# Moving the last two tiles' elementwise work of each up half from GpSimd to VectorE, placing the first down weights' low parts behind them, and reordering the last row scalings

## The chip, the core and the metric

The kernel runs on one core of a Trainium2 chip. The core has a matrix engine (TensorE, PE in the profile, with its weight loads listed as PEld), three engines for elementwise work (VectorE = DVE, ScalarE = ACT, GpSimd = POOL) and SyncE (SP), which here only issues transfers. Each engine works through its own queue in order; semaphores tie the queues together. The metric is the device time of one execution in microseconds. Three runs of the kernel before gave 871.04 us as their median (870.61 to 871.61).

## The reference: what is computed

One encoder block on a sequence of 512 tokens of width 1024, in float32: three token mixers merged by gates, then a feed-forward part and a final norm. The change touches the feed-forward part and the end:

```python
def conv_glu_ffn(h, w_up, w_conv, b_conv, w_down):
    a, u = jnp.split(h @ w_up, 2, axis=-1)
    return (jax.nn.gelu(dwconv3(a, w_conv, b_conv)) * u) @ w_down
...
        x = x + conv_glu_ffn(rms_norm(x, ffn_norm_g[l]), w_ffn_up[l], w_ffn_conv[l], b_ffn_conv[l], w_ffn_down[l])
    return rms_norm(x, final_norm_g)
```

`w_up` is 1024 x 5632 (2816 channels for `a`, 2816 for `u`), `w_down` is 2816 x 1024. `dwconv3` is a convolution of three taps along the tokens, channel by channel.

## The kernel before

**Products in three parts.** Every matrix product of float32 operands is made of three products of shorter numbers: each operand is split into a high part (ScalarE rounds it, line 242 for weights, 1304 for activations) and a low part (VectorE subtracts the high part, line 243 for weights, 1305 for activations). High by high, high by low and low by high are added up in PSUM: lines 260, 261, 262 where a weight is the stationary operand, lines 1255, 1256, 1257 in the down product.

**Weights.** They come as blocks of 128 x 1024 in the order of a list. SyncE loads a block into one of three `raw` buffers (`wr`, line 206). `emit_split` (line 223) splits it in two halves of 512 columns into four `hi` (`wh`) and four `lo` (`wl`) buffers. `weights(key)` splits one block ahead of the one it hands out and loads three ahead.

**The up half.** The 2816 channels are 22 tiles of 128, handled in two halves (`hh`) of 11 tiles (`j` = 0 to 10). For each tile TensorE makes the `a` product (24 matmuls of 512 columns) and then the `u` product (24 more). Meanwhile the other engines work on the `a` tile in a chain. `conv` multiplies it out of PSUM into a padded buffer (line 518, `pad`, the tile's first operation), and then come the three taps (line 520 on ACT, 521 and 522 on DVE). The gelu follows (1347 ACT, 1348 DVE, 1349 ACT, 1350 DVE), and then a multiplication by the rows' norm factor (line 1351), on GpSimd for the tiles 0 to 9 and on VectorE for tile 10. When the `u` product stands in PSUM, `gated` multiplies the two (line 1358, DVE), splits a half of the result (1304, 1305) and forms differences and sums of the two halves of the tokens: line 1361 in the first half, lines 1365, 1367 and 1368 in the second, all on GpSimd. The last tile's `gated` is put behind the first block of the down product that follows.

**The down products.** Seven products of half size (a scheme of the Strassen kind: B11 and T3 after the first half, B21, T1, T2, B22 and T4 after the second) each run over 11 tiles `k` of 128 channels and two groups of 128 tokens, with three matmuls of 512 columns each: 66 matmuls. One half block of weights, `wh` and `wl`, serves one `k`, which is six matmuls. B21 is the first product behind the second up half. Its weight blocks 0, 1 and 2 hold the tiles `k` = 0 and 1, 2 and 3, 4 and 5.

**The end.** T4 is the last product. While it runs, row groups 0 and 1 of the output are scaled and written (`finish`: a small addition at line 1286, a power at 1287 on GpSimd, two scalings at 1293 on VectorE, a transfer at 1300). With `hold=5`, T4 puts the last 15 matmuls on the bank of row group 3, so group 2's bank is complete before. Behind T4 come group 2 (line 1412 adds the bank, 1271 squares it on ACT, 1286, 1287, two scalings at 1293, transfer at 1417) and group 3 (1271, 1286, 1287, then 1421 on DVE and 1423 on ACT, with transfers at 1422 and 1424).

**Order.** Tile programs are queued engine by engine by a scheduler that works from the order of the code, readiness and explicit edges; `tc.issue_after(x)` keeps what a block emits on `x`'s engine behind `x` in that engine's queue, without a wait for its end.

Of the kernel before, what the change touches and what calls it, by code (L numbers as in the profile page):

```python
# [14 lines left out]
ALU = mybir.AluOpType  # L15
# [3 lines left out]
S = 512  # L19
D = 1024  # L20
# [5 lines left out]
HF = FT // 2  # L26
# [72 lines left out]
BLOCKS = block_list()  # L99
# [22 lines left out]
def hybrid_block(ctx, tc, xg, xT, memT, wflat, vecs, gbias, nabias, out):  # L122
# [99 lines left out]

    def emit_split(i):
        key, n = BLOCKS[i]
        r = raws.pop(i)
# [288 lines left out]
    def conv(ps, rbt, w, b, i, n):  # L514

        pad = pads[npad[0] % 2]
        npad[0] += 1
        V.tensor_tensor(pad[:, 1:513], ps, rbt, op=ALU.mult)  # L518
        t1 = scr()
# [798 lines left out]
    for hh in range(2):  # L1318
# [6 lines left out]
        for j in range(HF):  # L1325
# [24 lines left out]
            V.scalar_tensor_tensor(c, sq, 1.0, c, op0=ALU.add, op1=ALU.mult)  # L1350
            (V if j == HF - 1 else G).tensor_tensor(c, c, rb2, op=ALU.mult)  # L1351
            if f > 0:
                pu = pu1 if f == 1 else proj(("uu", f), HH, HL)

            def gated(j=j, pu=pu, c=c):

                r, q = (r1 if hh else r0)[j], r0[j]
                V.scalar_tensor_tensor(r, pu, 0.5, c, op0=ALU.mult, op1=ALU.mult)  # L1358
                if hh == 0:
                    split_half(a11, j, r[:, one_])  # L1360
                    G.tensor_tensor(r[:, one_], r[:, two_], r[:, one_], op=ALU.subtract)
                    late.append(lambda: split_half(s3, j, r[:, one_]))
                else:
                    split_half(a12, j, r[:, one_])
                    G.tensor_tensor(q[:, two_], q[:, two_], r[:, two_], op=ALU.subtract)
                    late.append(lambda: split_half(s1, j, q[:, two_]))
                    G.tensor_tensor(q[:, one_], q[:, one_], r[:, two_], op=ALU.subtract)
                    G.tensor_tensor(r[:, one_], r[:, one_], q[:, one_], op=ALU.add)

# [33 lines left out]
    def last_residual():  # L1403
# [4 lines left out]
        1: [lambda: gather(pc, 0, 1, ALU.add), lambda: ready(1, 0, 1)],  # L1408
        2: [last_residual],
        3: [lambda: finish(0, vs[0])],  # L1410
        4: [lambda: finish(1, vs[1]), lambda: V.tensor_tensor(cv(3, 1), cv(3, 1), gfin[:, S:D], op=ALU.mult)]})
    V.tensor_tensor(cv(2, 0), cv(2, 0), pa_[0], op=ALU.add)
    squares(cv(2, 0), 2, 0)
    col = power(2, vs[2], 0)
    scaled(2, 1, col)
    scaled(2, 0, col)
    SY.dma_start(out[2 * P:3 * P, :], C[1][:, :D])
    squares(pa_[1], 3, 0)
    col = power(3, vs[3], 0)
    oa, ob = scr(), scr()  # L1420
# [112 lines left out]
```

## Time and profile before

| | us |
|---|---|
| median of three runs | 871.04 (870.61 to 871.61) |
| the profiled execution, its own time | 870.92 |
| span of the profiled execution | 869.1 |
| busy: PE / DVE / ACT / POOL | 859.1 / 629.0 / 481.1 / 174.3 |
| second up half, its 11 tiles' first operations (line 518) | 667.22 to 781.49 |
| B21 / T1 begin on PE | 781.26 / 801.14 |
| last matmul begins | 861.66 |

The span is that of the engines' records; 1.82 us of the profiled execution's own time lie around it. TensorE is busy for 99% of the span, so time is to be had where it waits, where its clock is lowered, and behind the last matmul. A row of the timeline gives start, duration, engine, line, operation, the tiles written and read, and in brackets how long the engine was idle before and what ended that. Between matmuls in a row the starts lie 0.227 us apart though each is listed with 0.39 us, since they overlap.

### The profile page before, as it was taken

How to read it: one execution, taken by the hardware profiler on the slowest of the kernel's cores; microseconds unless marked ns; L12 is line 12 of the kernel's file. 1: busy time of each engine (PE TensorE's matmuls, PEld its weight loads, DVE VectorE, ACT ScalarE, POOL GpSimd, SP SyncE). 2: the span in 40 equal slices, each digit the busy share in tenths (PEclk: the TensorE clock that was granted, in tenths of full speed). 3: DMA queues.
4: the chain of work that ended last, by engine and by line, in shares of the span. 5: the costliest groups of instructions: out<-in, count | busy, mean ns of one | idle time of the engine just before them, and what ended most of it. 6: DMA issues, size and time to landing. Idle time of an engine off the chain costs nothing.

```text
span 869.1 us, 12209 instructions
## 1 busy us (share of the span) xinstructions
PE 859.1 (99%) x4175; PEld 722.8 (83%) x4175; DVE 629.0 (72%) x1255; ACT 481.1 (55%) x1023; POOL 174.3 (20%) x288
## 2 busy tenths in 40 slices
PE   9999999999999999999999999999999999998996
PEld 7898889988888888888888888888888888886885
DVE  7694687775567758898667549777776777777785
ACT  7363457654546658888634445555454444445763
POOL 0101100001013593700002103222200333331001
PEclk9999999999999999999999999999999999999998
DMA  7324633524485655633338956455556322225563
GB/s 277 100 74 141 205 127 116 190 86 134 158 194 130 206 157 155 165 112 110 108 99 208 326 167 146 161 178 148 145 180 194 97 98 80 91 97 183 186 204 141
DMA packets 42222, 131.93 MB, mean 152 GB/s; under 512 B 6376, under 2 KB 11496, under 8 KB 40560
## 3 DMA queue, kind: packets, MB, share of 16 engines
q1 hardware_dynamic: 32384, 101.37, 35.1%
q0 software_dynamic: 9344, 29.39, 14.0%
q8 instruction: 33, 0.54, 0.3%
q10 hardware_dynamic: 432, 0.39, 0.1%
q14 instruction: 29, 0.24, 0.1%
HBM read 126.91 MB, written 27.28 MB: 177 GB/s over the span
## 4 chain that ended last, share of the span: by engine, by line
PE 92%; DVE 3%; ACT 1%; POOL 1%; issue 1%; DMA 1%; POOLq 0%; DVEq 0%
PE mm L262 23%; PE mm L260 23%; PE mm L261 23%; PE at L1257 2%; PE at L1255 2%; PE at L1256 2%; PE at L261 2%; PE at L260 2%; PE at L262 2%; PE mm L1256 1%; PE mm L1257 1%; PE mm L1255 1%; PE at L934 1%; PE at L787 1%; PE at L915 1%
## 5 line engine op out<-in xcount | busy, mean ns | idle before, releaser
L260 PE MATMUL mm<-u,wh 128*128 128x512 f32 (+1 forms) x907 | 353.9, 390 | 0.0
L262 PE MATMUL mm<-u,wl 128*128 128x512 f32 (+1 forms) x907 | 350.2, 386 | 0.0
L261 PE MATMUL mm<-u,wh 128*128 128x512 f32 (+1 forms) x907 | 349.7, 386 | 0.0
L242 ACT ACTIVATE wh<-wr 128x512 fp32r<-128x512 f32 (+2 forms) x328 | 202.5, 624 | 167.4 <-PE mm L261 101.1
L243 DVE TENSOR_TENSOR wl<-wr,wh 128x512 fp32r<-128x512 f32 (+2 forms) x330 | 237.8, 724 | 73.6 <-ACT wh L242 69.7
L262 PEld LDWEIGHTS mm<-u,wl 128*128 128x128 f32 x907 | 170.4, 188 | 34.6
L261 PEld LDWEIGHTS mm<-u,wh 128*128 128x128 f32 x907 | 170.6, 188 | 32.8
L260 PEld LDWEIGHTS mm<-u,wh 128*128 128x128 f32 x907 | 170.5, 188 | 32.2
L600 POOL DMA_DIRECT2D u<-nav_d x128 | 62.8, 539 | 28.2 <-PE at L934 17.2
L1351 POOL TENSOR_TENSOR s<-s,rb 128x512 f32<-128x512 f32 x20 | 32.9, 1644 | 124.6 <-DVE s L1350 117.6
L169 POOL COPY y<-wl 128x1 f32<-128x1 f32 x24 | 6.9, 288 | 203.5 <-DVE wl L243 203.4
L1255 PE MATMUL at<-wh,u 128*128 128x512 f32 x100 | 39.3, 393 | 0.0
L1257 PE MATMUL at<-wh,u 128*128 128x512 f32 x100 | 38.9, 389 | 0.0
L1256 PE MATMUL at<-wl,u 128*128 128x512 f32 x100 | 38.9, 389 | 0.0
L1304 ACT ACTIVATE u<-r 128x256 fp32r<-128x256 f32 x44 | 17.7, 414 | 37.9 <-DVE r L1358 22.8
L520 ACT ACTIVATE s<-pad,vec 128x512 f32<-128x512 f32 x30 | 24.4, 812 | 17.5 <-DVE pad L518 16.8
L521 DVE SCALAR_TENSOR_TENSOR s<-pad,vec,s 128x512 f32<-128x512 f32 x30 | 22.9, 762 | 5.9 <-ACT s L520 5.8
L1347 ACT ACTIVATE s<-s 128x512 f32<-128x512 f32 x22 | 13.9, 633 | 21.7 <-DVE s L522 21.7
L1305 DVE TENSOR_TENSOR u<-r,u 128x256 fp32r<-128x256 f32 x44 | 21.0, 487 | 6.6 <-ACT u L1304 6.6
L1350 DVE SCALAR_TENSOR_TENSOR s<-s,s 128x512 f32<-128x512 f32 x22 | 15.2, 691 | 14.0 <-ACT s L1349 14.0
L522 DVE SCALAR_TENSOR_TENSOR s<-pad,vec,s 128x512 f32<-128x512 f32 x30 | 22.5, 751 | 0.8
L1349 ACT ACTIVATE s<-s 128x512 f32<-128x512 f32 x22 | 13.9, 632 | 15.5 <-DVE s L1348 15.4
(319 smaller groups left out, 1250.6 us busy)
## 6 DMA issues: line engine op xcount, KB each, us to landing
wr<-wflat SPq DMA_DIRECT2D x140, 512.0 KB, 3.4
wr<-wsum_T SPq DMA_DIRECT2D x20, 512.0 KB, 4.0
wsum_T<-wflat POOLq DMA_DIRECT2D x8, 1024.0 KB, 10.5
wsum_T<-wflat POOLq DMA_DIRECT2D x6, 768.0 KB, 7.5
nab<-nabias SPq DMA_DIRECT2D x16, 256.0 KB, 2.7
u<-nav_d POOLq DMA_DIRECT2D x128, 32.0 KB, 2.8
s<-xT SPq DMA_DIRECT2D x15, 256.0 KB, 4.7
nav_d<-nv POOLq DMA_DIRECT2D x8, 256.0 KB, 2.5
```

The costliest lines, as they stand in the source:

```text
L242: st["hi"] = A.activation(h[:, u:v], src, AF.Copy).ins
L243: st["lo"] = V.tensor_tensor(l[:, u:v], src, h[:, u:v].bitcast(F32), op=ALU.subtract).ins
L260: PE.matmul(ps, lh, rh, start=start, stop=False)
L261: PE.matmul(ps, lh, rl, start=False, stop=False)
L262: st["mm"] = PE.matmul(ps, ll, rh, start=False, stop=stop).ins
L520: A.activation(t1, pad[:, 0:512], AF.Identity, scale=vcol(w, i), bias=vcol(b, i))
L521: V.scalar_tensor_tensor(t1, pad[:, 1:513], vcol(w, n + i), t1, op0=ALU.mult, op1=ALU.add)
L600: G.dma_start(vw[r * 32:(r + 1) * 32, i * 256:(i + 1) * 256], nav_v[hf, r, CW[b]:CW[b] + 32, hp * 256:(hp + 1) * 256])
L1255: PE.matmul(bank, ah[:, ts], w[0], start=start, stop=False, skip_group_check=True)
L1256: PE.matmul(bank, ah[:, ts], w[1], start=False, stop=False, skip_group_check=True)
L1257: PE.matmul(bank, al[:, ts], w[0], start=False, stop=True, skip_group_check=True)
L1351: (V if j == HF - 1 else G).tensor_tensor(c, c, rb2, op=ALU.mult)
```

## The change

Three edits.

First, in both halves the tiles 9 and 10 do all their elementwise work on VectorE: the multiplication by the norm factor (tile 10 had it there), and the differences and sums in `gated`, one instruction a tile in the first half, three in the second.

Second, the weight blocks 0 of B11 and of B21 are split under `issue_after` of the newest `pad` instruction. At that point it is that of tile 10, so both low parts of the block stand behind it in VectorE's queue.

Third, near the end `finish(0)` and `finish(1)` stand one weight block of T4 earlier, and the squares and the small addition of row group 3 are written ahead of the second scaling of group 2, which is kept behind that addition.

```diff
     def emit_split(i):
+        if BLOCKS[i][0] in (("dn", "B11", 0), ("dn", "B21", 0)):
+            with tc.issue_after(st["pad"]):
+                split_block(i)
+        else:
+            split_block(i)
+
+    def split_block(i):
         key, n = BLOCKS[i]
...
-        V.tensor_tensor(pad[:, 1:513], ps, rbt, op=ALU.mult)
+        st["pad"] = V.tensor_tensor(pad[:, 1:513], ps, rbt, op=ALU.mult).ins
...
-            (V if j == HF - 1 else G).tensor_tensor(c, c, rb2, op=ALU.mult)
+            ve = V if j >= HF - 2 else G
+            ve.tensor_tensor(c, c, rb2, op=ALU.mult)
...
                 if hh == 0:
                     split_half(a11, j, r[:, one_])
-                    G.tensor_tensor(r[:, one_], r[:, two_], r[:, one_], op=ALU.subtract)
+                    ve.tensor_tensor(r[:, one_], r[:, two_], r[:, one_], op=ALU.subtract)
                     late.append(lambda: split_half(s3, j, r[:, one_]))
                 else:
                     split_half(a12, j, r[:, one_])
-                    G.tensor_tensor(q[:, two_], q[:, two_], r[:, two_], op=ALU.subtract)
+                    ve.tensor_tensor(q[:, two_], q[:, two_], r[:, two_], op=ALU.subtract)
                     late.append(lambda: split_half(s1, j, q[:, two_]))
-                    G.tensor_tensor(q[:, one_], q[:, one_], r[:, two_], op=ALU.subtract)
-                    G.tensor_tensor(r[:, one_], r[:, one_], q[:, one_], op=ALU.add)
+                    ve.tensor_tensor(q[:, one_], q[:, one_], r[:, two_], op=ALU.subtract)
+                    ve.tensor_tensor(r[:, one_], r[:, one_], q[:, one_], op=ALU.add)
...
-        2: [last_residual],
-        3: [lambda: finish(0, vs[0])],
-        4: [lambda: finish(1, vs[1]), lambda: V.tensor_tensor(cv(3, 1), cv(3, 1), gfin[:, S:D], op=ALU.mult)]})
+        2: [last_residual, lambda: finish(0, vs[0])],
+        3: [lambda: finish(1, vs[1])],
+        4: [lambda: V.tensor_tensor(cv(3, 1), cv(3, 1), gfin[:, S:D], op=ALU.mult)]})
     V.tensor_tensor(cv(2, 0), cv(2, 0), pa_[0], op=ALU.add)
     squares(cv(2, 0), 2, 0)
-    col = power(2, vs[2], 0)
-    scaled(2, 1, col)
-    scaled(2, 0, col)
+    col2 = power(2, vs[2], 0)
+    scaled(2, 1, col2)
+    squares(pa_[1], 3, 0)
+    col = tiny(1)
+    first = V.tensor_tensor(col, ss[3][:, 0:1], vs[3], op=ALU.add).ins
+    G.tensor_tensor(col, col, nhalf[:, :1], op=ALU.pow)
+    with tc.issue_after(first):
+        scaled(2, 0, col2)
     SY.dma_start(out[2 * P:3 * P, :], C[1][:, :D])
-    squares(pa_[1], 3, 0)
-    col = power(3, vs[3], 0)
```

The new lines shift the numbers: line 243 of before is 250 after, 518 is 525, 1305 is 1312, 1348 and 1350 are 1355 and 1357, 1351 is 1359, 1358 is 1366, 1365, 1367 and 1368 are 1373, 1375 and 1376, 1286 is 1293, 1293 is 1300, 1411 and 1412 are 1419 and 1420, 1421 is 1432.

The order of the instructions on TensorE and SyncE is the same in both kernels. Three places on VectorE show what moves. The first is VectorE's queue of before, at the end of tile 9 and the start of tile 10 of the second half (`mm_7709` is tile 9's `u` product, `mm_7750` tile 10's `a` product, `wl_7791` and `wl_7795` are the low parts of B21's block 0):

```order
L243 TENSOR_TENSOR wl_7747<-wr_7651,wh_7746 128x512
L1358 SCALAR_TENSOR_TENSOR u_6838<-mm_7709,s_7689 128x512
L1305 TENSOR_TENSOR u_6841<-u_6838,u_6841 128x256
L1305 TENSOR_TENSOR u_6844<-r_5536,u_6844 128x256
L243 TENSOR_TENSOR wl_7791<-wr_7699,wh_7790 128x512
L518 TENSOR_TENSOR pad_153<-mm_7750,rb_5621 128x512
L243 TENSOR_TENSOR wl_7795<-wr_7699,wh_7794 128x512
```

The same place after the change:

```order
L1359 TENSOR_TENSOR s_7689<-s_7689,rb_5621 128x512
L250 TENSOR_TENSOR wl_7747<-wr_7651,wh_7746 128x512
L1366 SCALAR_TENSOR_TENSOR u_6838<-mm_7709,s_7689 128x512
L1373 TENSOR_TENSOR r_5536<-r_5536,u_6838 128x256
L1375 TENSOR_TENSOR r_5536<-r_5536,u_6838 128x256
L1312 TENSOR_TENSOR u_6841<-u_6838,u_6841 128x256
L1376 TENSOR_TENSOR u_6838<-u_6838,r_5536 128x256
L1312 TENSOR_TENSOR u_6844<-r_5536,u_6844 128x256
L525 TENSOR_TENSOR pad_153<-mm_7750,rb_5621 128x512
L250 TENSOR_TENSOR wl_7791<-wr_7699,wh_7790 128x512
L250 TENSOR_TENSOR wl_7795<-wr_7699,wh_7794 128x512
```

Four instructions have come over from GpSimd, and `wl_7791` has moved from ahead of the `pad` instruction to behind it. On ScalarE one row has moved here: the high part `wh_7790` now stands between the two of line 1304.

The second place is VectorE's queue some rows further on, inside tile 10's chain, before (`wl_7835` and `wl_7839` are the low parts of B21's tiles `k` = 2 and 3, `wl_7857` that of `k` = 4):

```order
L243 TENSOR_TENSOR wl_7835<-wr_7740,wh_7834 128x512
L1348 SCALAR_TENSOR_TENSOR s_7782<-s_7782,s_7778 128x512
L1350 SCALAR_TENSOR_TENSOR s_7778<-s_7782,s_7778 128x512
L1351 TENSOR_TENSOR s_7778<-s_7778,rb_5621 128x512
L243 TENSOR_TENSOR wl_7839<-wr_7740,wh_7838 128x512
L243 TENSOR_TENSOR wl_7857<-wr_7788,wh_7856 128x512
```

And after:

```order
L250 TENSOR_TENSOR wl_7835<-wr_7740,wh_7834 128x512
L1355 SCALAR_TENSOR_TENSOR s_7782<-s_7782,s_7778 128x512
L1357 SCALAR_TENSOR_TENSOR s_7778<-s_7782,s_7778 128x512
L250 TENSOR_TENSOR wl_7839<-wr_7740,wh_7838 128x512
L1359 TENSOR_TENSOR s_7778<-s_7778,rb_5621 128x512
L250 TENSOR_TENSOR wl_7857<-wr_7788,wh_7856 128x512
```

The low part `wl_7839` now precedes the multiplication by the norm factor. The third place is the end of VectorE's queue, before, from `finish(0)`'s scalings on (`u_8442` is the last weight tile of T4, `at_6580` and `at_6581` are T4's two banks, `y_8512` and `y_8520` the row factors of groups 2 and 3):

```order
L1293 SCALAR_TENSOR_TENSOR u_5525<-u_5525,y_8464,u_7830 128x512 x2
L243 TENSOR_TENSOR u_8442<-wr_8438,u_8442 128x512
L1286 TENSOR_TENSOR y_8478<-sv 128x1
L1411 TENSOR_TENSOR u_5526<-u_5526,u_7830 128x512
L1293 SCALAR_TENSOR_TENSOR u_5525<-u_5525,y_8478,u_7830 128x512 x2
L1412 TENSOR_TENSOR u_5526<-u_5526,at_6580 128x512
L1286 TENSOR_TENSOR y_8512<-sv 128x1
L1293 SCALAR_TENSOR_TENSOR u_5526<-u_5526,y_8512,u_7830 128x512 x2
L1286 TENSOR_TENSOR y_8520<-sv 128x1
L1421 SCALAR_TENSOR_TENSOR s_8523<-at_6581,y_8520,u_7830 128x512
```

And after:

```order
L1300 SCALAR_TENSOR_TENSOR u_5525<-u_5525,y_8448,u_7830 128x512 x2
L1293 TENSOR_TENSOR y_8470<-sv 128x1
L250 TENSOR_TENSOR u_8442<-wr_8438,u_8442 128x512
L1300 SCALAR_TENSOR_TENSOR u_5525<-u_5525,y_8470,u_7830 128x512 x2
L1419 TENSOR_TENSOR u_5526<-u_5526,u_7830 128x512
L1420 TENSOR_TENSOR u_5526<-u_5526,at_6580 128x512
L1293 TENSOR_TENSOR y_8512<-sv 128x1
L1300 SCALAR_TENSOR_TENSOR u_5526<-u_5526,y_8512,u_7830 128x512
L1426 TENSOR_TENSOR y_8518<-sv 128x1
L1300 SCALAR_TENSOR_TENSOR u_5526<-u_5526,y_8512,u_7830 128x512
L1432 SCALAR_TENSOR_TENSOR s_8523<-at_6581,y_8518,u_7830 128x512
```

Group 1's small addition stands ahead of the last weight tile, group 3's stands between the two scalings of group 2.

More of the change, by code (lines that the diff above doesn't have):

```diff
@@ L1350, in hybrid_block, with gated @@
             V.scalar_tensor_tensor(c, sq, 1.0, c, op0=ALU.add, op1=ALU.mult)
-            (V if j == HF - 1 else G).tensor_tensor(c, c, rb2, op=ALU.mult)
+            ve = V if j >= HF - 2 else G
+            ve.tensor_tensor(c, c, rb2, op=ALU.mult)
             if f > 0:
                 pu = pu1 if f == 1 else proj(("uu", f), HH, HL)
-            def gated(j=j, pu=pu, c=c):
+            def gated(j=j, pu=pu, c=c, ve=ve):
                 r, q = (r1 if hh else r0)[j], r0[j]
```

## The prediction

> **What bounds the kernel now.** I read the page first, then who TensorE waited for, then the timeline of two products, then the chain of waits.
>
> ```profile
> PE 859.1 (99%) x4175; PEld 722.8 (83%) x4175; DVE 629.0 (72%) x1255; ACT 481.1 (55%) x1023; POOL 174.3 (20%) x288
> PE mm L1256 <- DVE wl L243: 1.7, 2, 1.0
> PE mm L1255 <- ACT wh L242: 0.5, 1, 0.5
> ```
>
> TensorE sets the time. It waits at only a few places, and behind the start of the program they all lie in the products of the down part: 2.2 us by this list. The list is too small, as two products of equal shape show. B11 (first and last fence row below: its start and T3's) and B21 (its start and T1's) are 66 matmuls each:
>
> ```profile
> 631.66 0.39 PE L1255 MATMUL at<-wh,u 128*128 128x512 f32 x1
> 646.62 0.39 PE L1255 MATMUL mm<-wh,u 128*128 128x512 f32 x1
> 781.26 0.39 PE L1255 MATMUL mm<-wh,u 128*128 128x512 f32 x1
> 801.14 0.39 PE L1255 MATMUL at<-wh,u 128*128 128x512 f32 x1
> ```
>
> B11 takes 646.62 - 631.66 = 14.96 us, 0.2267 per matmul. B21 takes 19.88. So **4.92 us** are lost inside B21, and its rows say where:
>
> ```profile
> 781.63 0.50 PE L1256 MATMUL mm<-wl,u 128*128 128x512 f32 x1
> 785.25 0.50 PE L1256 MATMUL mm<-wl,u 128*128 128x512 f32 x1 [0.61 <-DVE wl L243]
> 785.59 0.40 PE L1257 MATMUL mm<-wh,u 128*128 128x512 f32 x1
> 787.23 0.50 PE L1255 MATMUL mm<-wh,u 128*128 128x512 f32 x1 [0.54 <-ACT wh L242]
> 788.76 0.64 PE L1256 MATMUL mm<-wl,u 128*128 128x512 f32 x1 [1.04 <-DVE wl L243]
> 792.18 0.49 PE L1255 MATMUL mm<-wh,u 128*128 128x512 f32 x1
> 788.00:789.00 1.00, 0.24 (x1) 0.24 (x2) 1.00 (x3) 0.73 (x2) 0.00 (x0) 0.98 0.00 0
> 792.00:793.00 1.00, 1.00 (x5) 0.77 (x5) 0.82 (x2) 0.67 (x2) 0.92 (x2) 0.81 0.40 148
> ```
>
> Count the matmuls of B21 from 0. Number 1 (781.63) should start at 781.49: 0.25 lost with the slower restart behind it. Number 13 (785.25) waits for the low part of k = 2, number 18 (787.23) for the high part of k = 3, number 19 (788.76) for its low part. With the restarts, 0.34 us to the next start where 0.23 is usual (785.25 to 785.59), these three cost 2.9. Then the clock falls. The granted clock is 0.98 in the microsecond before 789 and 0.81 in the one before 793, with half speed between, so about 788.97 to 792.38. The 8 intervals from 788.76 to 792.18 take 3.42 us in place of 1.81: 1.6 lost, and 0.1 behind.
>
> Why are the weights late? VectorE's chain per tile is longer than TensorE's work on a tile:
>
> ```profile
> 747.33 0.61 DVE pad L518
> 758.75 0.61 DVE pad L518
> ```
>
> These rows of the chain of waits stand 11.42 us apart, while 48 matmuls take 10.88. Ten such steps put tile 10's first operation at 781.49, after B21 has begun. This is the stretch that the change edits (tile 9's end, then tile 10):
>
> ```profile
> 775.28 0.69 DVE L1350 SCALAR_TENSOR_TENSOR s<-s,s 128x512 f32<-128x512 f32 x1 [0.70 <-ACT s L1349]
> 776.05 1.67 POOL L1351 TENSOR_TENSOR s<-s,rb 128x512 f32<-128x512 f32 x1 [6.44 <-DVE s L1350]
> 777.75 0.69 DVE L1358 SCALAR_TENSOR_TENSOR u<-mm,s 128x512 f32<-128x512 f32 x1 [1.18 <-POOL s L1351]
> 778.52 0.73 POOL L1365 TENSOR_TENSOR r<-r,u 128x256 f32<-128x256 f32 x1 [0.81 <-DVE u L1358]
> 779.21 0.93 POOL L1367 TENSOR_TENSOR r<-r,u 128x256 f32<-128x256 f32 x1
> 779.74 0.68 DVE L1305 TENSOR_TENSOR u<-r,u 128x256 fp32r<-128x256 f32 x1 [0.20 <-ACT u L1304]
> 780.34 1.23 DVE L243 TENSOR_TENSOR wl<-wr,wh 128x512 fp32r<-128x512 f32 x1
> 781.49 0.68 DVE L518 TENSOR_TENSOR pad<-mm,rb 128x512 f32<-128x512 f32 x1
> 783.06 0.75 DVE L521 SCALAR_TENSOR_TENSOR s<-pad,vec,s 128x512 f32<-128x512 f32 x1 [0.29 <-ACT s L520]
> 784.51 0.68 DVE L243 TENSOR_TENSOR wl<-wr,wh 128x512 fp32r<-128x512 f32 x1
> 786.56 2.17 ACT L242 ACTIVATE wh<-wr 128x512 fp32r<-128x512 f32 x4
> 786.69 0.69 DVE L1350 SCALAR_TENSOR_TENSOR s<-s,s 128x512 f32<-128x512 f32 x1 [0.70 <-ACT s L1349]
> 787.41 0.69 DVE L1351 TENSOR_TENSOR s<-s,rb 128x512 f32<-128x512 f32 x1
> 788.02 1.89 DVE L243 TENSOR_TENSOR wl<-wr,wh 128x512 fp32r<-128x512 f32 x3
> 627.28 0.43 DVE L1305 TENSOR_TENSOR u<-r,u 128x256 fp32r<-128x256 f32 x1
> ```
>
> **The change, part by part.**
>
> *First edit, second half.* GpSimd's multiplication takes 1.67 and holds VectorE's queue for 1.18; tile 10 has the same one on VectorE, 0.69 (787.41). The three sums of 128x256 have no VectorE row here. The nearest is a subtraction of that shape: 0.43 with GpSimd idle (627.28, first half), 0.68 with GpSimd at work (779.74). GpSimd has nothing left to do here, so I take 0.43; starts in a row then lie about 0.36 apart. If each costs 0.68, everything behind is 0.75 later; I see no reason for less than 0.43.
>
> Replay from 775.28, with 0.61 between independent operations of 512 columns and 0.72 between dependent ones, as in these rows: the multiplication at 776.00, low part of the `u` weights 776.61, L1358 777.24, the two subtractions 777.96 and 778.33, the first low part of activations 778.70, the sum 779.06. The second low part needs ScalarE, where a weight's high part now stands between; it is ready at 779.4, so 779.45. Tile 10's `pad` starts at **779.81**, 1.68 earlier than 781.49. Its input was finished at about 776.0 (24 matmuls before 781.26 the `u` product starts), so no new wait stands there.
>
> *Second edit.* Both low parts of block 0 are now behind `pad`: 780.41 and 781.03. The first ends at 781.09, and number 1 wants it at 781.49, so the 0.25 goes. Queued behind them, L521 comes at 781.66, 1.40 before its old 783.06 (ScalarE's tap is ready 1.57 behind `pad`, as 783.06 was behind 781.49, so by 781.4). From there the chain is as before: low part of k = 2 at 783.11 to 783.79 (wanted at 784.21: that wait goes, by a margin of 0.4), the high parts from 785.16, L1350 at 785.29.
>
> *The order in tile 10's chain.* The low part of k = 3 now precedes the multiplication: it starts at 785.92 and ends at 786.59, 2.1 before its old 788.70. Number 18 would be due at 785.34 and waits for its high part until 785.83; number 19 starts at 786.65 and number 20 at 786.99 where 785.79 was due. So **1.20 us** stay lost. The rest keeps ahead: the low part of k = 4 ends at 787.81 (wanted 788.12), of k = 5 at 788.4 (789.5), of k = 7 at 791.4 (792.2). T1's first block is loaded into the buffer that k = 7's low part frees then:
>
> ```profile
> wr<-wsum_T SPq DMA_DIRECT2D x20, 512.0 KB, 4.0
> ```
>
> With 4.0 us to landing it is there at about 795.5 and, 0.6 and 0.7 for its two parts, split by 796.8; it is wanted at 797.6.
>
> In the worst stretch of 3.41 us TensorE then starts matmuls for (3.41 - 1.20) / 3.41 = 65% of the time. Before, the 3.41 us that ended at 788.97 had six starts (numbers 14 to 19) of 0.2267, 40%, and the clock fell; the 3.41 us before had eleven (3 to 13), 73%, and the clock stayed. 65% is nearer to 73, so I take the full clock. Gain in B21: 4.92 - 1.20 = **3.7 us**.
>
> *First half.* B11 lost nothing, so its earlier chain gains nothing. Its first low part moves behind `pad`, which follows the row of 627.28, and is wanted 0.2 behind 631.66: cover of about 3 us. The other loads follow TensorE through their buffers and move with it.
>
> *Third edit.*
>
> ```profile
> 859.86 0.68 DVE L1412 TENSOR_TENSOR u<-u,at 128x512 f32<-128x512 f32 x1
> 862.09 0.60 ACT L1271 ACTIVATE s<-at 128x512 f32<-128x512 f32 x1 [0.79 <-PE at L1257]
> 862.15 1.41 DVE L1293 SCALAR_TENSOR_TENSOR u<-u,y,u 128x512 f32<-128x512 f32 x2 [0.66 <-POOL y L1287]
> 863.48 0.15 DVE L1286 TENSOR_TENSOR y<-sv 128x1 f32<-128x1 f32 x1
> 863.60 0.33 SPq L1417 DMA_DIRECT2D out<-u  x1
> 865.08 0.33 SPq L1422 DMA_DIRECT2D out<-s  x1
> 865.50:866.00 0.50, 0.00 (x0) 0.00 (x0) 0.00 (x0) 0.00 (x0) 0.00 (x0) 0.50 0.52 201
> ```
>
> Group 3's squares are done at 862.8, but its addition waits behind both scalings of group 2 until 863.48. Group 2's bank is complete 15 matmuls before T4's end (861.66 starts the last), at about 858.7, but is added at 859.86, behind `finish(1)`'s scalings. These now stand a block earlier, so the addition of the bank comes about 1 us sooner, group 2's first scaling is through by 861.9, and group 3's small addition starts at 862.8: 0.67 earlier. Group 2's transfer (863.60) stays, since its second scaling now follows that addition. The two transfers of group 3 would be issued at 864.4, while group 2's still moves data: the half microsecond to 866.0 is half empty (201 GB/s), so only this gap of 0.25 can close, with a little at the end. I take **0.3**, between 0 and 0.67.
>
> *Sum.* 870.92 (the profiled execution: span 869.1 and 1.82 around it) - 3.7 - 0.3 = 866.9. The median of the runs is 871.04, 0.12 higher: **867.0**.
>
> **The rivals.**
>
> *A: the clock falls all the same.* For: the boundary lies between 40 and 73%, and 1.2 us of waiting stand in one place. Against: 65% is near the upper end. One window costs half of 3.41: 867.0 + 1.7 = 868.7. The Trainium skill bears on this ("TensorE: Matmul & The Clock Gate", section "What's actually happening"): the clock is halved after an idle window of about 3.4 us, windows that run freely. By that rule alone the changed kernel keeps its clock, as in my forecast. The trace agrees on the length but not on "idle": the window that cost the clock held six matmuls and no pause over 1.04 us.
>
> *B: the wait moves.* VectorE now works without a pause from 785 to 792, with margins of 0.3 at k = 4 and 0.8 at T1's first weights. If the sums cost 0.68, `pad` is 0.75 later, and so are k = 3 and k = 4: 867.8; with a late T1 load 868.5.
>
> *C: it does not carry to the end, or not happen.* If `wh` for k = 2 and 3 is held by ScalarE's or the loads' order and not by `pad`, B21 loses what it lost and only the end gains: 870.7. Against: L521 and L1347 to L1350 follow `pad` at fixed distances for tile after tile.
>
> *D: slower, by VectorE's queue.* If the four operations cost on VectorE what they cost on GpSimd (1.67, 0.73, 0.93, and for the last an estimate of 0.8 between those two), `pad` starts at 782.45. Block 0's low parts, now behind it, stop TensorE at number 1 for 2.3 us, so that a second window falls under 40% and costs 1.7, and k = 3 comes 0.5 later than before: 870.7 + 0.5 + 1.7 = 872.9. It decides from a `pad` start of about 782.0 on. The row of 0.69 speaks against it.
>
> **How the numbers follow.** Forecast 0.63 (its own 866.2 to 867.8), A 0.14, B 0.12, C 0.07, D 0.04. The low end takes in that k = 3's wait goes too (867.0 - 1.2 = 865.8), the high end A with a little: 865.8 to 868.9. A measurement here can tell 0.2%, 1.7 us, from no change: faster is below 869.3. That holds the forecast, A and B but for a tail of 0.02: faster 0.87, within 0.09, slower 0.04.
>
> **What would show it.** Tile 10's `pad` some 1.5 us before B21's start; B21 taking about 16.2 us in place of 19.88, with one wait, at k = 3; granted clock 1.00 throughout B21; group 3's addition between group 2's scalings, and the two last transfers 0.7 closer to group 2's. A granted clock of 0.5 in B21, a second wait at k = 4 or at T1's start, or a `pad` after 780.5 on this clock would make it wrong.

## The result, and the profile after

| | before | after |
|---|---|---|
| median of the runs, us | 870.88 (869.97 to 871.67, 6 runs) | 867.41 (867.16 to 868.33, 6 runs) |
| profiled execution, us (span) | 870.92 (869.14) | 867.16 (865.39) |
| start of B11, us from the span's start | 631.66 | 631.89 |
| B11, 66 matmuls | 14.96 | 14.96 |
| start of B11 to start of B21 | 149.60 | 149.60 |
| B21, 66 matmuls | 19.88 | 16.06 |
| start of T1 to last matmul | 60.53 | 60.53 |
| last matmul to the span's end | 7.48 | 7.31 |

The ratio is 0.9962, with a 95% interval of 0.9949 to 0.9975. The stages of the table are differences between starts of matmuls in the timeline; for the last stage the spans are taken from the traces to a hundredth, where the page gives a tenth. They add up to the change of the span: +0.23 - 3.82 + 0.00 - 0.17 = -3.76, and the execution's own time fell by as much. So about 1.78 us, and not 1.82, lie around the span, in both executions. Two stages differ by more than 0.2: B21, which the change is about, and the start of B11, ahead of which only the first half's edits lie. With those edits alone it starts at 632.68, no later than in the second execution of the kernel before (632.78), so they do not delay it; the last section shows what goes with it. Beside the experiments below, one run of the kernel before took 953.08 us at a mean granted clock of 0.85, and it counts in no ratio and in no group of the last section.

The page's busy times after the change, with the number of instructions:

```profile
PE 857.2 (99%) x4175; PEld 721.9 (83%) x4175; DVE 628.6 (73%) x1265; ACT 481.2 (56%) x1023; POOL 165.0 (19%) x278
```

Ten instructions have moved from GpSimd to VectorE (1255 to 1265, 288 to 278): the multiplications of the two tiles 9, and the sums of four tiles, one each in the first half and three each in the second. What TensorE waits for (time in all, number, longest):

```profile
PE mm L1263 <- DVE wl L250: 0.3, 1, 0.3
PE mm L1262 <- ACT wh L249: 0.2, 1, 0.2
```

Of the 2.2 us of listed waits in the down products 0.5 remain. The timeline of TensorE shows where they stand, with B21's first row and T1's first around them:

```profile
781.49 0.39 PE L1262 MATMUL mm<-wh,u 128*128 128x512 f32 x1
785.35 0.39 PE L1264 MATMUL mm<-wh,u 128*128 128x512 f32 x1
785.95 0.51 PE L1262 MATMUL mm<-wh,u 128*128 128x512 f32 x1 [0.21 <-ACT wh L249]
786.76 0.50 PE L1263 MATMUL mm<-wl,u 128*128 128x512 f32 x1 [0.30 <-DVE wl L250]
787.10 0.39 PE L1264 MATMUL mm<-wh,u 128*128 128x512 f32 x1
797.55 0.39 PE L1262 MATMUL at<-wh,u 128*128 128x512 f32 x1
```

Nearly all that is lost in B21 is lost at k = 3: 785.95 stands 0.60 behind 785.35, where 0.23 is usual, 786.76 another 0.81 behind, 787.10 another 0.34. That is 1.07 of the 16.06 - 14.96 = 1.10. VectorE's timeline shows the new queue at work, from tile 9's multiplication to the low parts of k = 3 and behind:

```profile
776.26 0.69 DVE L1359 TENSOR_TENSOR s<-s,rb 128x512 f32<-128x512 f32 x1
778.19 0.42 DVE L1373 TENSOR_TENSOR r<-r,u 128x256 f32<-128x256 f32 x1
778.53 0.42 DVE L1375 TENSOR_TENSOR r<-r,u 128x256 f32<-128x256 f32 x1
779.32 0.42 DVE L1376 TENSOR_TENSOR u<-u,r 128x256 f32<-128x256 f32 x1
779.99 0.68 DVE L525 TENSOR_TENSOR pad<-mm,rb 128x512 f32<-128x512 f32 x1
780.60 1.28 DVE L250 TENSOR_TENSOR wl<-wr,wh 128x512 fp32r<-128x512 f32 x2
783.24 0.68 DVE L250 TENSOR_TENSOR wl<-wr,wh 128x512 fp32r<-128x512 f32 x1
785.41 0.69 DVE L1357 SCALAR_TENSOR_TENSOR s<-s,s 128x512 f32<-128x512 f32 x1 [0.70 <-ACT s L1356]
786.02 0.69 DVE L250 TENSOR_TENSOR wl<-wr,wh 128x512 fp32r<-128x512 f32 x1
786.62 0.68 DVE L1359 TENSOR_TENSOR s<-s,rb 128x512 f32<-128x512 f32 x1
```

The sums take 0.42, `pad` starts 1.50 before B21 (0.23 behind it in the kernel before), both low parts of block 0 follow it, and the low part of k = 3 (786.02) stands ahead of the multiplication. The windows of the trace give the granted clock as 1.00 over all of B21; in this one most of the waits stand (its columns are length, busy time of the engines with the number of instructions, clock, DMA share, GB/s):

```profile
783.41:786.82 3.41, 2.89 (x13) 1.84 (x11) 2.62 (x5) 2.65 (x5) 0.00 (x0) 1.00 0.73 287
```

At the end of the program the timeline of VectorE, GpSimd and SyncE reads, from group 3's small addition on:

```profile
859.23 0.16 DVE L1426 TENSOR_TENSOR y<-sv 128x1 f32<-128x1 f32 x1 [0.69 <-ACT s L1278]
859.30 0.74 DVE L1300 SCALAR_TENSOR_TENSOR u<-u,y,u 128x512 f32<-128x512 f32 x1
859.46 0.99 POOL L1427 TENSOR_TENSOR y<-y,nhalf 128x1 f32<-128x1 f32 x1 [1.72 <-DVE y L1426]
860.08 0.33 SPq L1430 DMA_DIRECT2D out<-u  x1
860.49 0.75 DVE L1432 SCALAR_TENSOR_TENSOR s<-at,y,u 128x512 f32<-128x512 f32 x1 [0.44 <-POOL y L1427]
861.27 0.33 SPq L1433 DMA_DIRECT2D out<-s  x1
```

The last matmul starts at 858.08. The addition comes 1.15 behind it, where it came 1.82 behind before (861.66 to 863.48): 0.67 gained. But the power that follows takes 0.99 in place of 0.55, so group 3's scaling is only 0.23 nearer to the last matmul (2.41 in place of 2.64) and the end 0.17.

### The profile page after: what moved, and what is told of

It reads as the page before. It is cut to its first block, busy times and chain, and to the rows that moved or that the text cites. A ratio compares the mean times of both kernels' runs of the same rounds, so it can differ in the third digit from the quotient of the medians.

```text
span 865.4 us, 12204 instructions
## 1 busy us (share of the span) xinstructions
PE 857.2 (99%) x4175; PEld 721.9 (83%) x4175; DVE 628.6 (73%) x1265; ACT 481.2 (56%) x1023; POOL 165.0 (19%) x278
## 4 chain that ended last, share of the span: by engine, by line
PE 93%; DVE 3%; ACT 1%; issue 1%; POOL 1%; DMA 1%; POOLq 0%
PE mm L267 23%; PE mm L269 23%; PE mm L268 23%; PE at L1264 2%; PE at L1262 2%; PE at L1263 2%; PE at L268 2%; PE at L267 2%; PE at L269 2%; PE mm L1263 1%; PE mm L1264 1%; PE mm L1262 1%; PE at L941 1%; PE at L794 1%; PE at L922 1%; DVE wl L250 1%
## 5 line engine op out<-in xcount | busy, mean ns | idle before, releaser
L250 DVE TENSOR_TENSOR wl<-wr,wh 128x512 fp32r<-128x512 f32 (+2 forms) x330 | 235.3, 717 | 75.4 <-ACT wh L249 69.9
L1359 POOL TENSOR_TENSOR s<-s,rb 128x512 f32<-128x512 f32 x18 | 29.6, 1646 | 113.0 <-DVE s L1357 106.0
```

Of the source, the lines that this page charges most:

```text
L250: st["lo"] = V.tensor_tensor(l[:, u:v], src, h[:, u:v].bitcast(F32), op=ALU.subtract).ins
L1359: ve.tensor_tensor(c, c, rb2, op=ALU.mult)
```

## The experiments

The theory: the gain is VectorE's chain in tile 10, which edits 1 and 2 bring forward together; the first half has no part in it and edit 3 next to none. The rivals asked for in turn: one edit does it alone; the three sums, not the multiplication, do it; the first half does it by buffers that come free; edit 3 does it; and the granted clock decides. Nine kernels and a second profile of the kernel before tell these apart; each is compared with runs of the kernel before on the same chip. "Lost" is the time of B21 above the 14.96 of B11.

| kernel | median, us | kernel before, us | ratio (95%) | B21 | last matmul to end |
|---|---|---|---|---|---|
| edit 1 alone | 869.84 | 870.77 | 0.9983 (0.9974 to 0.9993) | 17.04 | 7.89 |
| edit 2 alone | 869.12 | 870.77 | 0.9982 (0.9973 to 0.9990) | 17.13 | 7.42 |
| edit 2 and tile 9's multiplication | 867.92 | 870.77 | 0.9969 (0.9958 to 0.9980) | 16.61 | 7.74 |
| edits 1 and 2 | 867.43 | 871.23 | 0.9959 (0.9949 to 0.9969) | 16.08 | 7.49 |
| edits 1 and 2, first half only | 870.15 | 871.23 | 0.9991 (0.9979 to 1.0003) | 18.34 | 7.38 |
| edit 3 alone | 870.38 | 870.77 | 0.9996 (0.9988 to 1.0004) | 19.89 | 7.37 |
| all, old order of the last scalings | 867.42 | 871.37 | 0.9956 (0.9942 to 0.9969) | 16.29 | 6.80 |
| all, whole second half on VectorE | 866.19 | 871.37 | 0.9943 (0.9930 to 0.9955) | 14.96 | 7.30 |
| the last two together | 866.38 | 871.37 | 0.9943 (0.9931 to 0.9955) | 14.96 | 7.49 |
| kernel before, profiled again | 870.32 | 871.37 | one run | 18.28 | 7.35 |

In all of them B11 takes 14.96 and the way from its start to B21's 149.60. The B21 of the full change, of edits 1 and 2, and of the old order of the last scalings have the same code; they took 16.06, 16.08 and 16.29, so a difference of 0.2 between two profiled executions proves nothing.

**Edit 1 alone**, against the kernel before (the sums of the first half too):

```diff
-            (V if j == HF - 1 else G).tensor_tensor(c, c, rb2, op=ALU.mult)
+            ve = V if j >= HF - 2 else G
+            ve.tensor_tensor(c, c, rb2, op=ALU.mult)
...
-                    G.tensor_tensor(q[:, two_], q[:, two_], r[:, two_], op=ALU.subtract)
+                    ve.tensor_tensor(q[:, two_], q[:, two_], r[:, two_], op=ALU.subtract)
...
```

> The first edit alone (tiles 9 and 10 on VectorE), the weights' low parts and the end as before. Theory (the gain in B21 is what is taken off the waits for the low and high parts of k = 2 and 3, and what the clock does with it): the first low part of block 0 stands ahead of tile 10's pad again, which therefore starts 0.6 later than in the changed kernel, and the low part of k = 3 stands behind the multiplication: by the rows about 2.2 us stay lost in B21, so 2.7 gained, about 868.2 us. With 2.2 us of one window missing the granted clock may fall in some executions (then 869.9). Rival G (GpSimd's slowness and its clash with VectorE are what cost the time; the order of the low parts adds nothing): the whole 3.7 us, 867.3. Rival O (the order of the low parts is everything): no change, 870.9.

Measured: 869.84 (868.29 to 870.93). B21 takes 17.04, so 2.08 are lost, and the clock stayed up in the profiled execution. TensorE's and VectorE's timelines of this kernel (`pad`, then the three low parts behind tile 10's multiplication, with the wait at T4 last):

```profile
781.29 0.69 DVE L518 TENSOR_TENSOR pad<-mm,rb 128x512 f32<-128x512 f32 x1
787.03 0.49 PE L1255 MATMUL mm<-wh,u 128*128 128x512 f32 x1 [0.44 <-ACT wh L242]
787.22 0.69 DVE L1352 TENSOR_TENSOR s<-s,rb 128x512 f32<-128x512 f32 x1
787.83 1.89 DVE L243 TENSOR_TENSOR wl<-wr,wh 128x512 fp32r<-128x512 f32 x3
788.57 0.50 PE L1256 MATMUL mm<-wl,u 128*128 128x512 f32 x1 [1.04 <-DVE wl L243]
857.09 0.50 PE L1256 MATMUL at<-u,u 128*128 128x512 f32 x1 [0.66 <-DVE u L243]
```

B21 starts at 782.33 here and `pad` 1.04 before it. That takes away the waits at the numbers 1 and 13. The wait of 1.04 at k = 3 stays as long as before, since its low part still follows the multiplication (787.22, then 787.83). The median is 1.6 above the 868.2 of the expectation, which counted from the execution of before in which the clock fell. The last experiment below gives 18.28 for B21 where it doesn't, and from there the gain is 1.24, near the 0.93 between the medians. In this execution TensorE also waited 0.66 for the low part of T4's last weights, at 857.09, and the way from T1 to the last matmul took 61.53 in place of 60.53; whether the edit has a part in that stays open.

**Edit 2 alone**, against the kernel before:

```diff
     def emit_split(i):
+        if BLOCKS[i][0] in (("dn", "B11", 0), ("dn", "B21", 0)):
+            with tc.issue_after(st["pad"]):
+                split_block(i)
+        else:
+            split_block(i)
...
```

> The second edit alone (block 0's low parts behind tile 10's pad), all sums on GpSimd as before. Theory: pad starts at about 780.3 instead of 781.5, and the order that comes with it puts the low part of k = 3 ahead of the multiplication: about 1.7 us stay lost in B21, 3.2 gained if the clock holds, about 867.7 us (869.4 if it falls). Rival G: no gain, 870.9, since GpSimd's operations are all still there. Rival O: the whole gain, 867.2.

Measured: 869.12 (868.02 to 870.24); 2.17 lost where 1.7 was expected. The timeline of TensorE, GpSimd and VectorE shows three places: number 1 (start at 781.56 for a B21 that starts at 781.14), k = 3, and one that was not expected, k = 7. The row of 791.63 is the low part of k = 7:

```profile
781.56 0.50 PE L1263 MATMUL mm<-wl,u 128*128 128x512 f32 x1
786.99 0.50 PE L1263 MATMUL mm<-wl,u 128*128 128x512 f32 x1 [0.31 <-DVE wl L250]
789.42 1.12 POOL L1372 TENSOR_TENSOR r<-r,u 128x256 f32<-128x256 f32 x1 [8.52 <-DVE u L1365]
789.86 0.96 DVE L1312 TENSOR_TENSOR u<-u,u 128x256 fp32r<-128x256 f32 x1
791.51 0.80 POOL L1375 TENSOR_TENSOR u<-u,r 128x256 f32<-128x256 f32 x1
791.63 1.22 DVE L250 TENSOR_TENSOR wl<-wr,wh 128x512 fp32r<-128x512 f32 x1
792.91 0.50 PE L1263 MATMUL mm<-wl,u 128*128 128x512 f32 x1 [0.18 <-DVE wl L250]
```

The order at k = 3 is the new one, and its loss falls to 1.30. With tile 10's sums left on GpSimd, VectorE's operations beside them take longer, the subtraction at 789.86 0.96 in place of 0.42 and the low part of k = 7 itself 1.22 in place of 0.68. It comes late: 0.5 lost. So the move of the sums pays, although the sums themselves are not what TensorE waits for. As with edit 1 alone, the expectation of 867.7 counted from a fallen clock; from 18.28 B21 gains 1.15.

**Edit 2 with tile 9's multiplication only** (the sums of both tiles stay on GpSimd), against the kernel before, beside the diff of edit 2:

```diff
-            (V if j == HF - 1 else G).tensor_tensor(c, c, rb2, op=ALU.mult)
+            (V if j >= HF - 2 else G).tensor_tensor(c, c, rb2, op=ALU.mult)
```

> The second edit, and of the first only the multiplication of tile 9 by the norm factor on VectorE; the sums stay on GpSimd, the end as before. Theory: the three sums lie beside other work here, so pad starts where it does in the changed kernel, about 779.8 to 780.0, and about 1.2 us stay lost in B21: 867.2 us. Rival: the sums on GpSimd clash with VectorE's low parts (each operation with two inputs in SBUF then takes 0.2 to 0.5 longer) and delay pad by half a microsecond or more: 867.8 and above.

Measured: 867.92 (867.54 to 868.58) where 867.2 was expected, and 1.65 lost: 1.11 at k = 3, near the 1.07 of the full change, and 0.5 at k = 7 again, which the expectation did not have. `pad` starts 1.46 before B21 (780.47 and 781.93), so the delay that the rival names did not come, although the time lies in the rival's range. The multiplication of tile 9 brings what edit 2 alone lacks at number 1; at k = 3 the two differ by no more than executions of one B21 do. The sums bring the 0.5 at k = 7 and nothing else that the trace shows.

**Edits 1 and 2 without edit 3**, against the changed kernel (the end of the kernel before, with its order of the last scalings too):

```diff
-        2: [last_residual, lambda: finish(0, vs[0])],
-        3: [lambda: finish(1, vs[1])],
...
+        2: [last_residual],
+        3: [lambda: finish(0, vs[0])],
+        4: [lambda: finish(1, vs[1]), lambda: V.tensor_tensor(cv(3, 1), cv(3, 1), gfin[:, S:D], op=ALU.mult)]})
...
```

> Edits 1 and 2 together without edit 3 (the end as before). B21 is to take 16.06 us as with all three. By the theory that edit 3 moves little: the time from the last matmul to the span's end 7.4 us, as in the kernel before, and a median within 0.4 us of the full change's 867.4. If edit 3 carries a part of its own as the prediction has it: 867.7. If the finishes' old place costs more once the rest is earlier: 868 or more.

Measured: 867.43 (866.94 to 870.10), the same as with all three, with 16.08 for B21. Whatever edit 3 is worth, it is too small for these runs.

**Edits 1 and 2 in the first half only**, against the changed kernel (the end as in the kernel before):

```diff
-        if BLOCKS[i][0] in (("dn", "B11", 0), ("dn", "B21", 0)):
+        if BLOCKS[i][0] in (("dn", "B11", 0),):
...
-            ve = V if j >= HF - 2 else G
-            ve.tensor_tensor(c, c, rb2, op=ALU.mult)
+            ve = V if hh == 0 and j >= HF - 2 else G
+            (V if j == HF - 1 else ve).tensor_tensor(c, c, rb2, op=ALU.mult)
...
```

> Edits 1 and 2 in the first half only (tiles 9 and 10 there on VectorE, block 0 of B11 split behind pad); the second half and the end as before. By the theory that B11 had nothing to gain: B11 takes 14.96 us as before, B21 18.3 (19.9 if the clock falls in it), ratio to before within 0.2% of 1. If the first half carried part of the gain, by way of buffers that come free earlier: ratio 0.998 or less, and a shorter way from the start of B11 to that of B21 than 149.60 us.

Measured: 870.15 (869.08 to 872.29); the interval holds 1. B11 is the same and so is the way to B21; B21 takes 18.34. The first half's edits do nothing that these runs can tell.

**Edit 3 alone**, against the kernel before:

```diff
-        2: [last_residual],
-        3: [lambda: finish(0, vs[0])],
+        2: [last_residual, lambda: finish(0, vs[0])],
+        3: [lambda: finish(1, vs[1])],
...
-    scaled(2, 0, col)
+    squares(pa_[1], 3, 0)
+    col = tiny(1)
+    first = V.tensor_tensor(col, ss[3][:, 0:1], vs[3], op=ALU.add).ins
+    G.tensor_tensor(col, col, nhalf[:, :1], op=ALU.pow)
+    with tc.issue_after(first):
+        scaled(2, 0, col2)
...
```

> The third edit alone (the end), B21 as before. Theory, after the trace of the changed kernel (0.12 us less from the last matmul to the end of the span): 870.8, no change that this measurement can tell; group 3's power on GpSimd takes about 1.0 us, since group 2's second scaling runs on VectorE at the same time. Rival: the end gains the 0.3 of the prediction or the full 0.67 that group 3's addition comes earlier, 870.2 to 870.6.

Measured: 870.38 (869.76 to 871.20), no difference. The end is 0.11 shorter in the trace (the 0.12 of the expectation is from spans to a tenth; 0.17 is nearer), and the power takes 0.99 here too.

**All edits, but the old order of the last scalings** (only the earlier `finish(0)` and `finish(1)` of edit 3 stay), against the changed kernel:

```diff
-    squares(pa_[1], 3, 0)
-    col = tiny(1)
-    first = V.tensor_tensor(col, ss[3][:, 0:1], vs[3], op=ALU.add).ins
-    G.tensor_tensor(col, col, nhalf[:, :1], op=ALU.pow)
-    with tc.issue_after(first):
-        scaled(2, 0, col2)
+    scaled(2, 0, col)
...
```

> The changed kernel with only the earlier finish of row groups 0 and 1 left of the third edit: at the end both scalings of group 2 stand ahead of group 3's small addition again. Theory: in the changed kernel group 3's power on GpSimd took 0.99 instead of 0.55, because group 2's second scaling, put behind the addition, runs on VectorE beside it and both read SBUF. With group 2's chain one us earlier both of its scalings end when group 3's squares do, so nothing waits: power 0.55, the last issue 0.4 earlier, group 2's transfer 0.7 earlier; last matmul to end of span 6.9 instead of 7.3, 867.0 us. Rival: the reordering is needed (group 3's addition then starts 0.6 later): 7.5 or more, 867.6.

Measured: 867.42 (866.90 to 867.52), the same as the full change. The timeline shows what the order does:

```profile
857.69 1.42 DVE L1300 SCALAR_TENSOR_TENSOR u<-u,y,u 128x512 f32<-128x512 f32 x2 [0.66 <-POOL y L1294]
859.47 0.16 DVE L1293 TENSOR_TENSOR y<-sv 128x1 f32<-128x1 f32 x1 [0.36 <-ACT s L1278]
859.71 0.55 POOL L1294 TENSOR_TENSOR y<-y,nhalf 128x1 f32<-128x1 f32 x1 [2.05 <-DVE y L1293]
860.29 0.75 DVE L1429 SCALAR_TENSOR_TENSOR s<-at,y,u 128x512 f32<-128x512 f32 x1 [0.66 <-POOL y L1294]
```

The last matmul starts at 858.33. The addition follows 1.14 behind it, as early as with the new order, for the scalings of group 2 are done (859.11) before group 3's squares are (859.43). The power takes 0.55, and the scaling comes 1.96 behind the last matmul in place of 2.41. So once the finishes stand earlier, the reordering has nothing left to gain here and costs 0.45. One execution shows that; the medians do not.

**The whole second half on VectorE** (on top of all three edits), against the changed kernel:

```diff
-            ve = V if j >= HF - 2 else G
+            ve = V if hh or j >= HF - 2 else G
```

> The changed kernel with the elementwise work of all eleven tiles of the second half on VectorE. Theory (VectorE's chain of 11.42 us per tile against TensorE's 10.88, with GpSimd's multiplication in it, is why tile 10 is late): without GpSimd the chain is shorter than TensorE's work, every pad starts right behind its product, tile 10's pad starts at about 776 to 777, and B21 loses nothing: 14.96 us, 1.1 gained, 866.3 us. Rival: VectorE has no room (its queue gets 1.9 us more per tile) and falls behind, waits come up in the up half: 867.4 or slower.

Measured: 866.19 (866.15 to 866.54), as expected. On the same chip the kernel of the paragraph above, whose B21 is close to that of the full change, ran between 866.90 and 867.52: no run of the two overlaps. VectorE's and TensorE's rows show the first operations of the tiles 9 and 10 and the ends of B21:

```profile
765.44 0.69 DVE L525 TENSOR_TENSOR pad<-mm,rb 128x512 f32<-128x512 f32 x1 [0.59 <-PE mm L269]
776.32 0.69 DVE L525 TENSOR_TENSOR pad<-mm,rb 128x512 f32<-128x512 f32 x1 [1.13 <-PE mm L269]
781.56 0.39 PE L1262 MATMUL mm<-wh,u 128*128 128x512 f32 x1
796.52 0.39 PE L1262 MATMUL at<-wh,u 128*128 128x512 f32 x1
```

The tiles now stand 10.88 us apart, TensorE's own pace, in place of 11.42, and `pad` waits for TensorE. B21 takes 14.96: nothing is lost any more. This is the shortest kernel of the study, though the measurement does not part it from the next.

**Both of the last two together**, against the changed kernel:

```diff
-            ve = V if j >= HF - 2 else G
+            ve = V if hh or j >= HF - 2 else G
...
-    with tc.issue_after(first):
-        scaled(2, 0, col2)
+    scaled(2, 0, col)
...
```

> Both of the foregoing together. Theory: their gains lie in different stages and add up: B21 14.96 us, last matmul to end 6.9, 865.9 us. Rival: one takes from the other, 866.3 or above.

Measured: 866.38 (865.75 to 866.89), not the further 0.4 that was expected. In its profiled execution ScalarE began to split T4's last weights, for whose landing it waits, 8.66 us before the last matmul (848.55 and 857.21), and in the kernel with the old order alone 9.81 us before (848.52 and 858.33). Group 2's scalings then end at 859.13, behind group 3's squares (858.32) and no longer before them; group 3's addition queues behind the scalings (1.83 behind the last matmul), and its scaling comes 2.64 behind the last matmul, where the new order has 2.40 in the kernel above (857.04 to 859.44). So by these traces the better order hangs on when those weights land; in the full change and in the kernel above the split began 9.48 and 9.41 us before the last matmul.

**The kernel before, profiled again.** Its edit is none.

> The kernel before, profiled a second time. Theory of the clock (windows of 3.41 us that run freely against the program; a fall needs one window with few matmuls in it): the waits in B21 are where they were, 3.2 us up to number 19, but the granted clock falls behind them only if a window lies so that it holds them nearly all. In the first profile it did, and B21 took 19.88. Where it does not fall, B21 takes about 18.3 and the time is about 1.6 lower. Rival: the fall belongs to these waits wherever the windows lie: 19.9 again.

Measured: B21 took 18.28, with the same three waits and a granted clock of 1.00. TensorE's timeline (B21's start, the wait at k = 3, T1's start):

```profile
782.38 0.39 PE L1255 MATMUL mm<-wh,u 128*128 128x512 f32 x1
789.86 0.50 PE L1256 MATMUL mm<-wl,u 128*128 128x512 f32 x1 [1.03 <-DVE wl L243]
800.66 0.39 PE L1255 MATMUL at<-wh,u 128*128 128x512 f32 x1
```

The window in which that wait stands, with the granted clock third from the end:

```profile
789.00:790.00 1.00, 0.14 (x1) 0.14 (x2) 1.00 (x3) 0.83 (x2) 0.00 (x0) 1.00 0.00 0
```

So the 1.6 us that the half clock cost in the profile of before belong to some executions only. How that comes is read in the last section.

## Why the prediction held, step by step

- **Tile 10's first operation.** Replayed for 779.81 on the clock of before; it came at 779.99 on a clock that runs 0.23 later, 1.50 before B21 where 1.45 was worked out. The four operations cost what the nearest rows said (0.69, and 0.42 for the estimate of 0.43). Rival D, which had them at GpSimd's prices, is refuted by those rows, and rival B's condition (0.68 for each sum) with it. (Rival D's own sum was off: the four operations are 0.98, 0.30, 0.50 and 0.37 dearer at its prices, 2.15 in all, which puts `pad` at 781.96 and not at 782.45.)
- **The waits at numbers 1 and 13 go.** Both did. The runs of the single edits show that each edit takes away number 13's and that number 1 needs the multiplication moved: with edit 2 alone it still lost 0.3.
- **k = 3 keeps 1.20.** It kept 1.07, at exactly the two matmuls named (1.06 and 1.27 in the two other kernels with the same B21). That the order there decides is shown by edit 1 alone, where the low part stays behind the multiplication and the wait stays 1.04.
- **Nothing new at k = 4, k = 7 or T1.** None came. The margin at k = 7 is real but hangs on the sums: with them on GpSimd it turned into 0.5 lost. That is near rival B's mechanism, one block further on than it was put, in kernels that leave a part of the change out.
- **The clock holds.** It did, in all six runs as far as the mean clock tells it (0.997 to 0.999). Rival A needed a window with too few matmuls; the two windows around k = 3 held 13 and 12 starts, and none of 3.41 us, wherever it is put, holds fewer than 10.
- **First half: nothing.** The run with those edits alone bears it out.
- **Edit 3: 0.3.** This term was too large: 0.17 in the trace, of which chance may be a part: the same last matmuls and the same old end took 7.48 and 7.35 in the two executions of the kernel before. The addition did come 0.67 earlier. What took most of that back was not group 2's transfer, as the prediction put it, but the power, which grew from 0.55 to 0.99 beside group 2's second scaling. So the sign named for it, the two last transfers 0.7 closer to group 2's, did not come either: the issues moved from 1.48 apart (863.60 and 865.08) to 1.19 (860.08 and 861.27). Five runs or more of each kernel do not tell the edit from nothing.
- **The sum.** 867.0 was forecast, 867.41 measured. In the profiled executions the difference is +0.23 for a later start and +0.13 for edit 3's missing part, less 0.12 that B21 gained beyond the forecast: 867.16 in place of 866.9. One assumption of the sum was not sound: the 1.6 us of half clock were taken as part of every execution. Against the execution in which the clock held, B21 gained 18.28 - 16.06 = 2.2, not 3.8. That this cost the sum so little is luck: that execution also began B11 1.12 later, so that its time was only 0.60 below the one from which the sum starts. The runs of before whose mean clock is low lie 3.9 above the changed kernel's median, near the 3.8 between the two profiled executions, and the others 2.9 (871.35 and 870.35, last section). The 0.7 beyond 2.2 is not settled; a later start, as in that execution, would be enough for it.

Rival C, no gain in B21, is refuted by B21's 16.06.

## What to carry to other kernels

Two products of equal shape, of which one follows a busier stage, give the loss directly, where the list of waits shows less than half of it; and the loss is then found matmul by matmul, in the order of the queue that feeds it. A chain that takes 11.42 us for a tile on an engine whose neighbour needs 10.88 is late at the last tile by the sum of all the tiles: moving the last two tiles' work, with the low parts put behind `pad`, took 3.8 us off B21 in the profile, of which 1.6 were half clock, and moving the work of all of them took away the rest. Before a stall is priced with a lowered clock from one profile, profile the kernel a second time.

## What the runs showed of the hardware

**The clock's windows.** In the profile of before the clock fell at 788.97 and again, behind the last matmul, at 864.06, which the windows of the two executions of before show (the clock is third from the end; first the first execution, then the second, each with the microsecond in which the clock falls):

```profile
864.00:865.00 1.00, 0.00 (x0) 0.00 (x0) 0.70 (x1) 0.70 (x1) 0.27 (x1) 0.53 0.60 246
```

```profile
863.00:864.00 1.00, 0.00 (x0) 0.00 (x0) 0.34 (x2) 0.31 (x1) 0.55 (x1) 0.77 0.21 86
```

A mean of 0.53 is 0.06 us at full clock and the rest at half, so the fall is at 864.06; 0.77 gives 863.54. From 788.97 to 864.06 are 75.09 us, 22 times 3.413, and the fall in B21 lasted 3.41 (788.97 to 792.38). Counted back from the fall at the end in the same way, a boundary stood at 788.45 in the second execution. The window ending there has 8 starts of matmuls of the 15 that fit and the next one 9; in the first execution the window that ended at 788.97 had 6. The same stall was cut in two. The two other kernels with the B21 of before go the same ways: edit 3 alone, with a boundary at 789.04, had a window with 5 starts and fell, and the first-half edits alone, with a boundary at 788.39, had windows with 8 and 9 and did not. A window with 7 starts (edit 1 alone) was not followed by half clock. With 6 it went both ways: with edit 2 alone the window from 857.50 to 860.91, in which the matmuls end, had 6 starts, and its clock fell only at 864.33. So the limit lies at about 6 of 15 here, and the count of starts alone does not settle it. A fall needs no idle window, and here no two starts lay further apart than 1.53 us (787.23 and 788.76).

The Trainium skill ("TensorE: Matmul & The Clock Gate", section "What's actually happening") has windows of that length that run freely of the kernel's start, and a fall after an idle one. Length and free running agree with these numbers; "idle", if it means a window without matmuls, does not.

The same windows show at the program's start. One of TensorE's first matmuls of 512 columns, in the second execution of before and then in the first:

```profile
5.85 0.63 PE L261 MATMUL mm<-u,wh 128*128 128x512 f32 x1
```

```profile
5.04 0.40 PE L261 MATMUL mm<-u,wh 128*128 128x512 f32 x1
```

In the second they take 0.63 and start 0.43 apart until about 6.7 us; in the first they have 0.40 and 0.23 from 5.04 on. Boundaries counted back from 788.45 and 788.97 by 3.413 fall at 6.87 and 3.98, near these changes. In the profile after, whose clock falls at 860.94, the same count gives 4.28, and B11 starts at 631.89. In the two executions of before B11 starts at 632.78 and at 631.66: 1.12 lost early, 1.6 not lost in B21, so the two come out at 870.32 and 870.92. That the place of the windows sets both was not tried; in these two executions it goes with both, and so it does in the two other kernels (B11 at 631.66 with edit 3 alone, at 632.68 with the first-half edits alone). In the 55 runs of the kernel before that were timed beside the experiments the mean granted clock was 0.996 or less in 24 (median 871.35; the first execution's is 0.995) and 0.997 or more in 31 (median 870.35; the second's is 0.997). None of the 6 runs of the full change, nor of the 42 of the other kernels with edit 2 in the second half, is in the lower group. That the mean clock tells the fall in B21 was seen in profiled executions only.

**GpSimd beside VectorE.** The power on 128 x 1 took 0.54 to 0.57 us when it began with VectorE at rest or ahead of VectorE's operation, and 0.93 to 0.99 when it began inside one that reads two tiles of SBUF. It then ended 0.40 to 0.43 behind that operation's end. In the end shown above: 860.04 and 860.45. Earlier in the same kernel, around row group 1:

```profile
852.41 0.68 DVE L250 TENSOR_TENSOR u<-wr,u 128x512 fp32r<-128x512 f32 x1
852.58 0.94 POOL L1294 TENSOR_TENSOR y<-y,nhalf 128x1 f32<-128x1 f32 x1 [1.89 <-DVE y L1293]
```

These end at 853.09 and 853.52. The Trainium skill ("SBUF — State Buffer", section "Who interferes with whom") says that a VectorE instruction with two SBUF inputs contends with a GpSimd instruction that reads SBUF. These rows agree, though no power here began inside a VectorE operation with a single SBUF input, so that the second input decides is not shown. They show that even the smallest GpSimd step on a closing chain can pay for it: here 0.44 us of the 0.67 that edit 3 had won.
